# A four-layer trunk on one core: the product with the compressed values as one stacked 128-row pass, a bias table in fewer copies, small attention steps in other places

## The chip, the core and the metric

The kernel runs on one core of one Trainium2 chip. A core has five instruction queues that run beside each other: TensorE (PE, matrix products; the load of its stationary operand is listed apart as PEld), VectorE (DVE), ScalarE (ACT), GpSimd (POOL) and SyncE (SP, which here only issues DMAs). On chip there is SBUF, 128 partitions wide, and PSUM, where TensorE leaves its products. What is measured is the time of the one core in device microseconds; lower is better.

## The reference

A sequence of 256 positions of width 2048 passes two layers. Layer 0 is a gMLP mixer, a SwiGLU FFN (5632 wide) and a gated per-layer embedding. Then one set of keys and values is made for three attention branches. Layer 1 is the attention mixer with that set, and again an FFN and an embedding. All is float32. What the change touches is the attention with the compressed branch and the bias that every logit gets:

```python
def compress_blocks(t, pe, w1, w2):
    ...
    return jax.nn.gelu(flat @ w1) @ w2          # 15 blocks for each of 2 groups, 128 wide
...
lc = einsum('bghqd,bgkd->bghqk', qb, k_cmp) * scale + rel_bias_heads(rel_table, t[:, None] - cmp_end[None, :])
pc = softmax(where(mc, lc, NEG_INF)) * any(mc)
o_cmp = einsum('bghqk,bgkd->bghqd', pc, v_cmp)
...
out = gb[..., 0:1] * o_cmp + gb[..., 1:2] * o_slc + gb[..., 2:3] * o_win
```

There are 16 heads in 2 groups. A compressed key is a block of 32 positions at a stride of 16, so that there are 15 of them; the selected and the window branch see up to 256 positions here. The bias of a logit is a function of its distance and its head alone.

## The kernel before

**Products in three passes.** TensorE multiplies float32 numbers rounded to a shorter form (`F32R`). So that nothing is lost, both operands are split: ScalarE copies a number to the short form (the high part, `split`, line 117), VectorE subtracts that from the number (the rest, line 118), and `mm3` (lines 124 to 126) adds high by high, rest by high and high by rest in PSUM. Every weight block takes this way: SP loads it (`wraw`, line 172, tile `raw`), ScalarE and VectorE split it (`wh`, `wl`), TensorE uses it. In the narrow stream (mixers) four blocks of 512 KB are in flight, in the wide stream (FFN and embedding) blocks of 1 MB.

**Order.** `weave` emits a matrix product block by block and, after each block, the small attention steps that a table of strings names for this place (`PLAN`: `q3` is the product that makes the queries of heads 3 to 6, `|` parts its blocks). In it `kb0` to `kb7` and `vb0` to `vb7` are the blocks of the compression product for keys and values, `cT` the transposes ahead of them, `kh kk kt` and `vh vv` their ends, `kT` and `xT` transposes of keys and of the residual, `qT3` the transposes of the queries of the product `q3`, and `s5 t5 v5` the three steps of head 5: scores, transposes, values. A scheduler then interleaves the emitted instructions of each engine; each engine runs its own list strictly in that order and waits on semaphores.

**One head.** `scores`: nine matmuls, a DMA of the bias tile of the head (128 rows x 400, three buffers), and for each of six rows of logits one DVE and one ACT instruction; the probabilities times the gates stay in the tile `L`, 800 columns: window and selected, then 32 columns of the compressed branch (two blocks of queries, 16 each). `transposes`: eight of 128 x 128 into the PSUM banks `pa` and `pb`, which are split into `pah`, `pal`, `pbh`, `pbl`. `values`: the products with the values into the bank `pv`, two heads in one bank, the odd head ending it. The compressed branch is one `mm3` with 16 rows:

```python
mm3(po, VCh[:, g, :], VCl[:, g, :], bh[:16, par, 2:4].rearrange("p j s -> p (j s)"),
    bl[:16, par, 2:4].rearrange("p j s -> p (j s)"), False, False)
```

**The bias table.** In row p of a head's bias tile the table of that head is shifted by p. `prepare_bias` (line 349, near the end of the first mixer) writes the table of 16 heads x 528 numbers to DRAM (`d0`) and from there 128 copies of it, one for each partition (`bias_rep`, line 359). It is issued on SP's queue, in which the next entries are the loads of the first FFN's weights.

Of the kernel before, what the change touches and what calls it, by code (L numbers as in the profile page):

```python
# [16 lines left out]
SEQ = 256  # L17
# [16 lines left out]
RW = 528  # L34
SCALE = HD ** -0.5
# [47 lines left out]
def trunk_kernel(ctx: ExitStack, tc: tile.TileContext, a: dict, out: bass.AP):  # L83
# [27 lines left out]
    def f32v(t):  # L111
        return t.bitcast(F32)
# [224 lines left out]

    bias_rep = dram.tile([P, H, RW], F32, name="bias_rep")

# [9 lines left out]
    def prepare_bias(tbl, oh):  # L349

        rt = tp.tile([H, RW], F32, tag="t0", name="rt")
        for hs in (slice(0, RW // 2), slice(RW // 2, RW)):
# [7 lines left out]
                                            ap=[[0, P], [RW, H], [1, RW]]))  # L360
# [254 lines left out]
    with ExitStack() as bctx:  # L615
# [7 lines left out]
        VCh = bp.tile([16, G, HD], F32R, name="VCh")  # L623
        VCl = bp.tile([16, G, HD], F32R, name="VCl")
# [8 lines left out]
        def compress_steps(kv):  # L633
# [19 lines left out]
            def hidden():  # L653
                pt = gen_bank("hidT")
                for j in range(2):
                    nc.tensor.matmul(pt[:, j * 32:j * 32 + 30], st["hid"][:, j * P:(j + 1) * P], sel, start=True, stop=True)
                st["hidT"] = sm.tile([P, 2, 32], F32, tag="hidT", name="hidT_sb")
# [25 lines left out]
            def values():  # L683
                po = gen_bank("cmpo")
                vc = tp.tile([16, G, HD], F32, tag="t2", name="vc")
                nc.vector.memset(vc, 0.0)
                for g in range(G):
                    for j in range(2):
                        nc.tensor.matmul(po[:15, g * HD:(g + 1) * HD], st["hidT"][:, j, g * 15:(g + 1) * 15],
                               w2[:, 1, j, :], start=(j == 0), stop=(j == 1))  # L690
                nc.vector.tensor_copy(vc[:15], po[:15, :G * HD].rearrange("p (g d) -> p g d", g=G))
                split(VCh, VCl, vc)
# [77 lines left out]
        def attn_steps(h, qh, ql, e):  # L770
# [4 lines left out]
            def scores():  # L775
# [9 lines left out]
                nc.sync.dma_start(bias[:, :400], bass.AP(tensor=brv.tensor, offset=brv.offset + 127 + h * RW,  # L785
# [267 lines left out]
```

## Time and profile before

| | us |
|---|---|
| median of 3 runs (2242.64 to 2243.59) | 2242.7 |
| the profiled execution | 2247.32 |
| its span, from the first instruction to the last | 2245.4 |
| TensorE busy | 2224.8 (99%) |
| VectorE busy | 1775.4 (79%) |
| ScalarE busy | 1234.8 (55%) |

The profiled execution is some 4.6 us above the median of the timed ones; differences are worked out within the profile and then taken off the median. A matmul's record in the trace is longer than the time until the next one can start, since matmuls overlap: what one costs is read from the distance of two starts, not from its length.

### The profile page before, as it was taken

The page shows a single profiled execution, that of the slowest core. Times are in us where ns is not written, and L with a number is a line of the kernel's source. Part 1 is how long each engine was busy: PE and PEld are TensorE (multiplying, and loading weights), DVE is VectorE, ACT ScalarE, POOL GpSimd, SP SyncE. Part 2 cuts the span into 40 slices and gives each one's busy share as a digit, 9 for nine tenths or more (in the row PEclk, how much of TensorE's full clock was granted, in tenths as well). Part 3 has the DMA queues.
Part 4 walks back from the last instruction along what each step waited for, and adds up shares of the span by engine and source line. Part 5 has one row for each costly group of instructions (what it writes and reads, how often), then busy time and mean ns, then how long its engine had stood idle before and what let it go on. Part 6 is the DMA issues. An engine that isn't in the chain of part 4 may idle for free.

```text
span 2245.4 us, 26612 instructions
## 1 busy us (share of the span) xinstructions
PE 2224.8 (99%) x10311; PEld 1849.1 (82%) x10311; DVE 1775.4 (79%) x2032; ACT 1234.8 (55%) x1438; POOL 25.6 (1%) x26
## 2 busy tenths in 40 slices
PE   8999999999999999999999999999999999999999
PEld 7888878888888888888887998888888888888887
DVE  5566579998988999755667777699999998898654
ACT  7555455555555555455567666555555555555543
POOL 0000000000000000000000000000000000000000
PEclk9999999999999999999999999999999999999999
DMA  8666756566555556655557444556555656655553
GB/s 310 193 193 211 214 198 206 179 214 213 200 200 189 199 199 207 206 182 180 184 174 237 120 154 140 179 197 206 194 200 204 208 188 206 218 198 203 184 196 132
DMA packets 118570, 438.54 MB, mean 195 GB/s; under 512 B 9147, under 2 KB 11579, under 8 KB 117932
## 3 DMA queue, kind: packets, MB, share of 16 engines
q1 hardware_dynamic: 116924, 434.38, 57.8%
q10 hardware_dynamic: 1440, 2.20, 0.3%
q8 instruction: 81, 1.33, 0.2%
q14 instruction: 45, 0.37, 0.1%
q0 software_dynamic: 80, 0.26, 0.0%
HBM read 434.68 MB, written 6.46 MB: 196 GB/s over the span
## 4 chain that ended last, share of the span: by engine, by line
PE 91%; DVE 3%; DMA 3%; ACT 1%; issue 1%; POOL 0%; SPq 0%; DVEq 0%; ACTq 0%
PE p L125 12%; PE p L126 12%; PE p L124 12%; PE fo L126 7%; PE fo L124 7%; PE fo L125 7%; PE pg L126 3%; PE pg L124 3%; PE pg L125 3%; DVE wl L118 2%; DMA raw<-in_ffn_w_in 2%; PE v L124 1%; PE v L125 1%; PE v L126 1%; PE bo L124 1%; PE u L125 1%
## 5 line engine op out<-in xcount | busy, mean ns | idle before, releaser
L118 DVE TENSOR_TENSOR wl<-raw,wh 128x2048 fp32r<-128x2048 f32 (+5 forms) x513 | 876.2, 1714 | 324.3 <-ACT wh L117 322.4
L117 ACT ACTIVATE wh<-raw 128x2048 fp32r<-128x2048 f32 (+5 forms) x513 | 744.9, 1455 | 638.3 <-PE fo L126 144.0
L117 ACT ACTIVATE wh<-t 128x1024 fp32r<-128x1024 f32 x204 | 209.0, 1056 | 198.7 <-PE p L126 78.0
L118 DVE TENSOR_TENSOR wl<-t,wh 128x1024 fp32r<-128x1024 f32 x204 | 242.9, 1220 | 43.9 <-ACT wh L117 43.4
L124 PE MATMUL p<-wh,exh 128*128 128x512 f32 x470 | 183.0, 391 | 0.9 <-ACT wh L117 0.9
L125 PE MATMUL p<-wl,exh 128*128 128x512 f32 x470 | 183.4, 390 | 0.1
L126 PE MATMUL p<-wh,exl 128*128 128x512 f32 x470 | 183.3, 390 | 0.0
L125 PE MATMUL p<-wl,hF0h 128*128 128x512 f32 x418 | 163.5, 391 | 3.0 <-DVE wl L118 3.0
L125 PE MATMUL p<-wl,hF1h 128*128 128x512 f32 x418 | 162.9, 390 | 0.6 <-DVE wl L118 0.6
L126 PE MATMUL p<-wh,hF0l 128*128 128x512 f32 x418 | 162.8, 390 | 0.0
L126 PE MATMUL p<-wh,hF1l 128*128 128x512 f32 x418 | 162.4, 389 | 0.0
L124 PE MATMUL p<-wh,hF0h 128*128 128x512 f32 x418 | 161.7, 391 | 0.4 <-ACT wh L117 0.4
L124 PE MATMUL p<-wh,hF1h 128*128 128x512 f32 x418 | 161.2, 390 | 0.0
L124 PE MATMUL fo<-wh,aT0h 128*128 128x512 f32 x352 | 138.3, 393 | 0.0
L124 PE MATMUL fo<-wh,aT1h 128*128 128x512 f32 x352 | 138.2, 393 | 0.0
L126 PE MATMUL fo<-wh,aT1l 128*128 128x512 f32 x352 | 137.2, 390 | 0.0
L126 PE MATMUL fo<-wh,aT0l 128*128 128x512 f32 x352 | 137.2, 390 | 0.0
L125 PE MATMUL fo<-wl,aT1h 128*128 128x512 f32 x352 | 137.1, 390 | 0.0
L125 PE MATMUL fo<-wl,aT0h 128*128 128x512 f32 x352 | 137.1, 389 | 0.0
L490 DVE TENSOR_TENSOR t<-raw 128x1024 f32<-128x1024 f32 x102 | 124.3, 1219 | 5.6 <-DMA raw<-in_ffn_w_in 5.6
L124 PEld LDWEIGHTS p<-wh,exh 128*128 128x128 f32 x470 | 88.4, 188 | 21.0 <-ACT wh L117 2.9
L125 PEld LDWEIGHTS p<-wl,exh 128*128 128x128 f32 x470 | 88.4, 188 | 19.6 <-DVE wl L118 1.0
(282 smaller groups left out, 4183.2 us busy)
## 6 DMA issues: line engine op xcount, KB each, us to landing
raw<-in_ffn_w_in SPq DMA_DIRECT2D x176, 1024.0 KB, 4.9
raw<-in_ffn_w_out SPq DMA_DIRECT2D x88, 1024.0 KB, 5.0
raw<-in_ple_gate SPq DMA_DIRECT2D x32, 1024.0 KB, 4.9
raw<-in_a_w_in SPq DMA_DIRECT2D x63, 512.0 KB, 4.0
raw<-in_a_w_out SPq DMA_DIRECT2D x32, 512.0 KB, 4.2
raw<-in_b_w_out SPq DMA_DIRECT2D x32, 512.0 KB, 3.6
raw<-in_kv_w SPq DMA_DIRECT2D x24, 512.0 KB, 3.6
raw<-in_b_w_in SPq DMA_DIRECT2D x24, 384.0 KB, 3.7
```

What stands on the lines that cost most here:

```text
L117: nc.scalar.activation(hi, src, AF.Copy)
L118: nc.vector.tensor_tensor(lo, src, f32v(hi), ALU.subtract)
L124: nc.tensor.matmul(ps, lh, rh, start=start, stop=False)
L125: nc.tensor.matmul(ps, lh, rl, start=False, stop=False)
L126: nc.tensor.matmul(ps, ll, rh, start=False, stop=stop)
L490: nc.vector.tensor_tensor(t13, r[:, 1:3], r[:, 0:1].to_broadcast([P, 2, NC]), ALU.subtract)
```

## The change

It does three things. First, the compressed values are stacked: rows 0 to 31 hold the high part, rows 32 to 63 the rest, rows 64 to 95 the high part again (`VC`, made from three copies of the hidden layer, `rep`). The compressed probabilities are written three times into 96 columns of `L`, so that a transpose puts them into the same rows; there rows 0 to 63 of `bh` are high parts and rows 64 to 95 are overwritten with the rest. One matmul over 128 rows then adds the three products. For that VectorE gets one instruction more per head (32 x 256) while its `pbl` gets half as wide, and the factor on the compressed logits is 96 columns wide and not 32. The matmul stands last in the step. Second, `bias_rep` holds 32 copies and a head's bias tile comes with four DMAs of 32 rows. Third, the table of the order has the small steps at other places.

```diff
+BC = 32
...
-    "q0": "cT0 | cT1 |  kb0 kb1 | kb2 kb3 | kb4 | kb5 kb6 | kb7  | kh kk",
-    "q3": "kt vb0 | vb1 vb2 | qT0 vb3 | vb4 s0 vb5 | s1 vb6 | vb7 t0 | vh s2 | vv  v0",
+    "q0": "cT0 |  | kb0 kb1 | kb2 kb3 | cT1 kb4 | kb5 | kb6 kb7 | kh kk",
+    "q3": "vb0 | vb1 | qT0 kt vb2 vb3 s0 | vb4 vb5 | s1 vb6 | vb7 t0 | s2 | vh vv v0",
...
-    bias_rep = dram.tile([P, H, RW], F32, name="bias_rep")
+    bias_rep = dram.tile([BC, H, RW], F32, name="bias_rep")
...
         nc.sync.dma_start(bias_rep, bass.AP(tensor=d0v.tensor, offset=d0v.offset,
-                                            ap=[[0, P], [RW, H], [1, RW]]))
+                                            ap=[[0, BC], [RW, H], [1, RW]]))
...
+                    rep = st["rep"] = tp.tile([P, 2, G, P], F32, tag="t2", name="rep")
+                    nc.vector.memset(rep, 0.0)
+                    for j in range(2):
+                        nc.scalar.activation(rep[:, j].rearrange("p g (i m) -> p g i m", i=4)[:, :, :3, :15],
+                                             pt[:, j * 32:j * 32 + 30].rearrange("p (g m) -> p g m", g=G).unsqueeze(2)
+                                             .to_broadcast([P, G, 3, 15]), AF.Gelu_apprx_tanh)
...
-                vc = tp.tile([16, G, HD], F32, tag="t2", name="vc")
-                nc.vector.memset(vc, 0.0)
...
-                        nc.tensor.matmul(po[:15, g * HD:(g + 1) * HD], st["hidT"][:, j, g * 15:(g + 1) * 15],
-                               w2[:, 1, j, :], start=(j == 0), stop=(j == 1))
-                nc.vector.tensor_copy(vc[:15], po[:15, :G * HD].rearrange("p (g d) -> p g d", g=G))
-                split(VCh, VCl, vc)
+                        nc.tensor.matmul(po[:, g * HD:(g + 1) * HD], st["rep"][:, j, g, :],
+                                         w2[:, 1, j, :], start=(j == 0), stop=(j == 1))
+                pov = po[:, :G * HD].rearrange("p (g d) -> p g d", g=G)
+                nc.scalar.activation(VC, pov, AF.Copy)
+                nc.vector.tensor_tensor(VC[32:64], pov[32:64], f32v(VC[32:64]), ALU.subtract)
...
-                nc.sync.dma_start(bias[:, :400], bass.AP(tensor=brv.tensor, offset=brv.offset + 127 + h * RW,
-                                                         ap=[[H * RW - 1, P], [1, 400]]))
+                for p0 in range(0, P, BC):
+                    nc.sync.dma_start(bias[p0:p0 + BC, :400],
+                                      bass.AP(tensor=brv.tensor, offset=brv.offset + 127 - p0 + h * RW,
+                                              ap=[[H * RW - 1, BC], [1, 400]]))
...
-                nc.vector.tensor_tensor(LC, LC, rr[:, 4:6].unsqueeze(2).to_broadcast([P, 2, 16]), ALU.mult)
+                nc.vector.tensor_tensor(L[:, 512:608].rearrange("p (i b s) -> p i b s", i=3, b=2),
+                                        LC.unsqueeze(1).to_broadcast([P, 3, 2, 16]),
+                                        rr[:, 4:6].unsqueeze(1).unsqueeze(3).to_broadcast([P, 3, 2, 16]), ALU.mult)
...
-                split(pair["bh"][:, par].rearrange("p j s -> p (j s)"),
-                      pair["bl"][:, par].rearrange("p j s -> p (j s)"), pb)
+                bh = pair["bh"][:, par].rearrange("p j s -> p (j s)")
+                nc.scalar.activation(bh, pb, AF.Copy)
+                nc.vector.tensor_tensor(bh[64:96, SEQ:], pb[64:96, SEQ:], f32v(bh[64:96, SEQ:]), ALU.subtract)
+                nc.vector.tensor_tensor(pair["bl"][:, par].rearrange("p j s -> p (j s)"), pb[:, :SEQ],
+                                        f32v(bh[:, :SEQ]), ALU.subtract)
...
-                mm3(po, VCh[:, g, :], VCl[:, g, :], bh[:16, par, 2:4].rearrange("p j s -> p (j s)"),
-                    bl[:16, par, 2:4].rearrange("p j s -> p (j s)"), False, False)
...
+                nc.tensor.matmul(po, VC[:, g, :], bh[:, par, 2:4].rearrange("p j s -> p (j s)"),
+                                 start=False, stop=par == 1)
```

The change moves every line below it, so that `mm3` stands in lines 126 to 128 of the changed kernel. Three places show what becomes of the lists.

TensorE, the value step of the last head, before (`pv` is the bank of two heads, `pah` and `pbh` transposed probabilities, `bo` the next matrix product):

```order
L126 MATMUL pv<-pah,Vl 128x256
L124 MATMUL pv<-pbh,VCh 128x256
L125 MATMUL pv<-pbl,VCh 128x256
L126 MATMUL pv<-pbh,VCl 128x256
L124 MATMUL pv<-pbh,Vh 128x2x128
L125 MATMUL pv<-pbl,Vh 128x2x128
L126 MATMUL pv<-pbh,Vl 128x2x128
L124 MATMUL pv<-pbh,Vh 128x2x128
```

and in the changed kernel:

```order
L128 MATMUL pv<-pah,Vl 128x256
L126 MATMUL pv<-pbh,Vh 128x2x128
L127 MATMUL pv<-pbl,Vh 128x2x128
L128 MATMUL pv<-pbh,Vl 128x2x128
L126 MATMUL pv<-pbh,Vh 128x2x128
L127 MATMUL pv<-pbl,Vh 128x2x128
L128 MATMUL pv<-pbh,Vl 128x2x128
L874 MATMUL pv<-pbh,VC 128x256
L126 MATMUL bo_0_10566<-wh,oTh 128x512
```

Three entries with `VCh` and `VCl` are gone, one with `VC` stands at the end.

TensorE, in the product `q3`, where the queries of heads 0 to 2 are transposed (`qT`), before (`ph` is the compression product, `kcT` the transposed compressed keys):

```order
L647 MATMUL ph<-wh,T 128x256
L648 MATMUL ph<-wl,T 128x256
L894 MATMUL qT<-ident,q 128x128 x6
L647 MATMUL ph<-wh,T 128x256
L125 MATMUL q_0_8936<-wl,hBh 128x512
L126 MATMUL q_0_8936<-wh,hBl 128x512
```

and in the changed kernel:

```order
L128 MATMUL q_0_8935<-wh,hBl 128x512
L126 MATMUL q_1_8936<-wh,hBh 128x512
L127 MATMUL q_1_8936<-wl,hBh 128x512
L128 MATMUL q_1_8936<-wh,hBl 128x512
L914 MATMUL qT<-ident,q 128x128 x6
L688 MATMUL kcT<-ident,kc 128x30
L651 MATMUL ph<-wl,T 128x256
```

Between the end of `q0` and `qT` there now stand 36 matmuls of `q3` and 17 of `ph` (before 26 and 24), and `kcT`, which stood 30 matmuls ahead of `qT`, comes behind it. The scores of head 0 stood 38 matmuls behind `qT` and now stand 16 behind it.

SP, the loads for the last query product and the first blocks of `bo` (its weight is `in_b_w_out`), before:

```order
L172 DMA raw<-in_b_w_in 128x768 x2
L172 DMA raw<-in_b_w_out 128x1024 x4
L785 DMA bias<-bias_rep 128x400
L172 DMA raw<-in_b_w_out 128x1024
L785 DMA bias<-bias_rep 128x400
L172 DMA raw<-in_b_w_out 128x1024
L785 DMA bias<-bias_rep 128x400
```

and in the changed kernel:

```order
L174 DMA raw<-in_b_w_out 128x1024 x5
L797 DMA bias<-bias_rep 32x400 x6
L174 DMA raw<-in_b_w_out 128x1024
L797 DMA bias<-bias_rep 32x400 x4
L174 DMA raw<-in_b_w_out 128x1024 x2
L797 DMA bias<-bias_rep 32x400 x2
```

Where one bias load stood between two weight loads there now stand two to six pieces.

## Rows read from the trace of the kernel before

**Rows 1.** The profile's page: each engine's busy time, share of the span and instructions.

```profile
PE 2224.8 (99%) x10311; PEld 1849.1 (82%) x10311; DVE 1775.4 (79%) x2032; ACT 1234.8 (55%) x1438; POOL 25.6 (1%) x26
```

**Rows 2.** TensorE's waits over the whole span: who waited for whom, us in total, times, longest.

```profile
PE p L125 <- DVE wl L118: 3.7, 5, 1.8
PE qT L894 <- DVE q L882: 1.0, 1, 1.0
```

**Rows 3.** Stretches of the span: from:to, their length, busy time of PE, PEld, DVE, ACT, POOL with instructions, granted TensorE clock, DMA share, GB/s. The first lies at the start of the first FFN, the second holds the end of `q0` and all of `q3`, the third the products `q7` to `q13`, the fourth most of the blocks of `bo` that attention steps are woven into.

```profile
290.00:300.00 10.00, 7.72 (x30) 5.92 (x29) 8.53 (x11) 8.13 (x11) 0.00 (x0) 0.83 0.53 203
...
1170.00:1235.00 65.00, 61.53 (x355) 52.95 (x353) 48.59 (x99) 47.59 (x84) 3.20 (x2) 1.00 0.71 229
1235.00:1330.00 95.00, 95.00 (x602) 89.23 (x603) 75.07 (x235) 65.96 (x180) 4.91 (x3) 1.00 0.44 132
1330.00:1400.00 70.00, 69.89 (x369) 57.98 (x368) 50.20 (x120) 42.93 (x104) 1.64 (x1) 1.00 0.44 140
```

**Rows 4.** TensorE in order of time in the value step of the last head: start, us, line, rows*columns of the stationary operand, shape of the moving one.

```profile
1383.39 0.28 PE L125 MATMUL pv<-pal,Vh 128*128 128x256 f32 x1
1383.51 0.28 PE L126 MATMUL pv<-pah,Vl 128*128 128x256 f32 x1
1383.72 0.38 PE L124 MATMUL pv<-pbh,VCh 16*128 16x256 f32 x1
1383.94 0.27 PE L125 MATMUL pv<-pbl,VCh 16*128 16x256 f32 x1
1384.06 0.28 PE L126 MATMUL pv<-pbh,VCl 16*128 16x256 f32 x1
1384.26 0.39 PE L124 MATMUL pv<-pbh,Vh 128*128 128x256 f32 x1
1384.49 0.28 PE L125 MATMUL pv<-pbl,Vh 128*128 128x256 f32 x1
```

**Rows 5.** The instructions on the tile `VCh`, one group for all heads: count, ns min/median/max, first and last start.

```profile
L124 PE MATMUL pv<-pbh,VCh x16: 377/382/383, 1236.7 to 1383.7; 16*128 16x256 f32 x16
```

**Rows 6.** TensorE in order of time in the value step of head 1, in which a transpose (L822) stands between the 16-row matmuls; left out are those three and one of 128 rows.

```profile
1242.55 0.28 PE L126 MATMUL pv<-pah,Vl 128*128 128x256 f32 x1
...
1243.06 0.33 PE L822 MATMUL pa<-ident,L 128*128 128x128 f32 x1
...
1243.96 0.28 PE L125 MATMUL pv<-pbl,Vh 128*128 128x256 f32 x1
```

**Rows 7.** The way to the first FFN: SP's queue in order of time at the write of the bias copies, the list of DMA issues with KB and us from issue to landing, and, out of the chain of work that ended last, the load of FFN weights issued at 276.11 us (start, us until it landed).

```profile
267.52 0.57 SPq L359 DMA_DIRECT2D bias_rep<-d  x1
...
bias_rep<-d SPq DMA_DIRECT2D x1, 4224.0 KB, 18.5
...
276.11 13.21 DMA raw<-in_ffn_w_in
```

**Rows 8.** ScalarE and TensorE in order of time at the start of the first FFN; in brackets the idle time before and its releaser. `p` are the FFN's first products, `mT` the first transposes behind them.

```profile
285.43 0.63 ACT L233 ACTIVATE junk<-x_sb 128x512 f32<-128x512 f32 x1 [0.64 <-DVE x_sb L304]
289.41 1.92 ACT L117 ACTIVATE wh<-raw 128x2048 fp32r<-128x2048 f32 x1 [3.25 <-DMA raw<-in_ffn_w_in]
...
284.45 0.39 PE L124 MATMUL p<-wh,hF0h 128*128 128x512 f32 x1
...
289.89 1.04 PE L264 MATMUL xT<-ident,x_sb 128*128 128x128 f32 x8
291.38 0.50 PE L124 MATMUL p<-wh,hF0h 128*128 128x512 f32 x1 [0.45 <-ACT wh L117]
293.71 0.50 PE L125 MATMUL p<-wl,hF0h 128*128 128x512 f32 x1 [1.83 <-DVE wl L118]
...
335.83 1.03 PE L313 MATMUL mT<-ident,up 128*128 128x128 f32 x8
```

**Rows 9.** The same place in the second layer's FFN: the two loads issued at 1432.2 us (KB, us to landing), and TensorE from the first product to the first `mT`.

```profile
raw<-in_ffn_w_in SPq DMA_DIRECT2D x2, 1024.0 KB, 6.0
...
1440.54 0.39 PE L124 MATMUL p<-wh,hF1h 128*128 128x512 f32 x1
1440.77 0.39 PE L125 MATMUL p<-wl,hF1h 128*128 128x512 f32 x1
...
1487.46 1.03 PE L313 MATMUL mT<-ident,up 128*128 128x128 f32 x8
```

**Rows 10.** TensorE in order of time from the last matmul of `q0` to the query transposes.

```profile
1191.31 0.35 PE L126 MATMUL q<-wh,hBl 128*128 128x432 f32 x1
...
1198.85 0.21 PE L676 MATMUL kcT<-ident,kc 30*128 30x30 f32 x1 [0.19 <-DVE kc L672]
...
1204.89 1.14 PE L894 MATMUL qT<-ident,q 128*128 128x128 f32 x6 [0.96 <-DVE q L882]
```

**Rows 11.** VectorE's instructions on `pbl` and on `L` that the change alters, or that are nearest to its new ones: ns min/median/max, shapes.

```profile
L118 DVE TENSOR_TENSOR pbl<-pb,pbh x16: 670/681/685, 1227.4 to 1382.7; 128x512 fp32r<-128x512 f32 x16
...
L813 DVE TENSOR_TENSOR L<-L,rr x16: 405/418/420, 1220.0 to 1370.4; 128x256 f32<-128x256 f32 x16
L814 DVE TENSOR_TENSOR L<-L,rr x16: 173/184/186, 1220.3 to 1370.7; 128x32 f32<-128x32 f32 x16
```

**Rows 12.** The instructions on the tile `bias`: SP's issue of one load (ns), and us from issue to landing.

```profile
L785 SPq DMA_DIRECT2D bias<-bias_rep x16: 326/327/425, 1092.7 to 1330.5; - x16
...
DMA to landing us min/median/max: 2.4/2.5/5.6
```

More of the change, by code (lines that the diff above doesn't have):

```diff
@@ L622, in trunk_kernel @@
         Vl = bp.tile([P, 2, TT, G, HD], F32R, name="Vl")
-        VCh = bp.tile([16, G, HD], F32R, name="VCh")
-        VCl = bp.tile([16, G, HD], F32R, name="VCl")
+        VC = bp.tile([P, G, HD], F32R, name="VC")
         brv = bias_rep[:, :, :]
@@ L656, in hidden @@
                     nc.tensor.matmul(pt[:, j * 32:j * 32 + 30], st["hid"][:, j * P:(j + 1) * P], sel, start=True, stop=True)
+                if kv == 1:
+                    rep = st["rep"] = tp.tile([P, 2, G, P], F32, tag="t2", name="rep")
[4 more added lines that the diff above has]
+                                             .to_broadcast([P, G, 3, 15]), AF.Gelu_apprx_tanh)
+                    return
                 st["hidT"] = sm.tile([P, 2, 32], F32, tag="hidT", name="hidT_sb")
@@ L784, in scores @@
                 bias = at.tile([P, 416], F32, tag="bias", name="bias", align_bytes=128, bufs=3)
-                nc.sync.dma_start(bias[:, :400], bass.AP(tensor=brv.tensor, offset=brv.offset + 127 + h * RW,
-                                                         ap=[[H * RW - 1, P], [1, 400]]))
-                L = at.tile([P, 800], F32, tag="L", name="L", align_bytes=128)
+                for p0 in range(0, P, BC):
+                    nc.sync.dma_start(bias[p0:p0 + BC, :400],
+                                      bass.AP(tensor=brv.tensor, offset=brv.offset + 127 - p0 + h * RW,
+                                              ap=[[H * RW - 1, BC], [1, 400]]))
+                L = at.tile([P, 896], F32, tag="L", name="L", align_bytes=128)
                 L1 = L[:, :512].rearrange("p (k b s) -> p k b s", k=2, b=2)
-                LC = L[:, 512:544].rearrange("p (b s) -> p b s", b=2)
-                L0 = L[:, 544:800].rearrange("p (b s) -> p b s", b=2)
+                LC = L[:, 864:896].rearrange("p (b s) -> p b s", b=2)
+                L0 = L[:, 608:864].rearrange("p (b s) -> p b s", b=2)
                 s1v = s1.rearrange("p (k b s) -> p k b s", k=2, b=2)
@@ L821, in transposes @@
                 for b in range(2):
-                    nc.tensor.transpose(pa[:, b * SEQ:b * SEQ + P], L[:, 544 + b * P:544 + (b + 1) * P], ident)
+                    nc.tensor.transpose(pa[:, b * SEQ:b * SEQ + P], L[:, 608 + b * P:608 + (b + 1) * P], ident)
                     nc.tensor.transpose(pa[:, b * SEQ + P:(b + 1) * SEQ], L[:, b * P:(b + 1) * P], ident)
@@ L829, in transposes @@
                     pair["bh"] = at.tile([P, 2, 4, P], F32R, tag="pbh", name="pbh", align_bytes=128, bufs=1)
-                    pair["bl"] = at.tile([P, 2, 4, P], F32R, tag="pbl", name="pbl", align_bytes=128, bufs=1)
+                    pair["bl"] = at.tile([P, 2, 2, P], F32R, tag="pbl", name="pbl", align_bytes=128, bufs=1)
                 st["pah"] = pah = at.tile([P, 2, SEQ], F32R, tag="pah", name="pah", align_bytes=128)
@@ L855, in values @@
                         mm3(pb_out, Vh[:, b, 1, g, :], Vl[:, b, 1, g, :], bh[:, :, b], bl[:, :, b],
-                            False, b == 1)
+                            False, False)
+                nc.tensor.matmul(po, VC[:, g, :], bh[:, par, 2:4].rearrange("p j s -> p (j s)"),
+                                 start=False, stop=par == 1)
+                if par == 1:
                     split(oT[0][:, h - 1:h + 1, :].rearrange("p k s -> p (k s)"),
```

12 rows, old and new, of the table PLAN are left out of this document.

## The prediction

> **What bounds the kernel now.** I began with the page. TensorE is busy in 2224.8 us, 99% of the span [rows 1]; the others have slack on average. So time can be won in two ways only: fewer or shorter slots on TensorE, and the few places where it stands still. Next I read its waits over the whole span: the longest entries after the start-up are short, 3.7 us in five pieces in the first products of the FFN and 1.0 us at the query transposes [rows 2]. Then the windows, stage by stage. In the attention part, 1235 to 1330 us, TensorE has no idle time, VectorE is busy 75.07 of 95 and ScalarE 65.96; between 1330 and 1400 it is 69.89 of 70 [rows 3]. Between 1170 and 1235 TensorE is busy 61.53 of 65: here work waits. And at 290 to 300 us it is busy 7.72 of 10, at a granted clock of 0.83 where nearly everywhere else it is 1.00 [rows 3]. The change has a part in each of these places.
>
> A busy TensorE hides one thing that the timeline shows: how far apart two starts lie. That is the price of a matmul here, and with it I cost the first part.
>
> **The stacked product.** In the last head's value step, 128-row matmuls of 256 columns start 0.12 us apart (1383.39, 1383.51). Then come the three 16-row ones. The first starts 0.21 later, the second 0.22 after it, the third 0.12, and the next two 128-row ones after 0.20 and 0.23 [rows 4]. Going to the short operand and back each costs about 0.2 us over the plain distance. From 1383.51 to 1384.49 are 0.98 us; two of the starts in it are 128-row matmuls at 0.12. So the three compressed passes cost 0.98 - 0.24 = 0.74 us, although their columns are worth 0.36. There are 16 such groups, one per head [rows 5]: 16 x 0.74 = 11.8. In three heads the lists put another matmul between the 16-row ones, which makes one more change each way. In head 1 the stretch is 1.41 us [rows 6], of which three foreign starts are 0.34: 1.07, that is 0.33 more. Three such heads add 1.0. In all 12.8 us. The new pass has 128 rows like its neighbours, so neither change is left: 16 x 0.12 = 1.9. The term is 1.9 - 12.8 = **-10.9 us**. Its bounds: if the new pass, the last of its group, still cost a change on one side (0.2), it would be 16 x 0.2 = 3.2 less, -7.7; if all foreign matmuls were dearer than I count them, -11.9.
>
> The Trainium skill (TensorEngine Tiling (Array Packing), Performance Considerations, When to Use Tiling) advises the opposite of stacking for a contract dimension of 32 or less: four row tiles side by side. By that the three 16-row passes would be worth about one pass, and making them one full pass would win next to nothing. The row differs: these three read the same rows 0 to 15, start 0.22 and 0.12 us apart and not together, and pay at both ends.
>
> What the new form adds lies on VectorE. `pbl` took 0.681 us at 512 columns [rows 11]; it becomes two instructions. No row shows either: at half of it they are 0.68 together, and with each at the 0.418 of a 256-column instruction 0.84, so 0 to 0.16 more. The factor on the compressed logits goes from 32 to 96 columns, between 0.184 and 0.418 [rows 11], on the line between them 0.25. So at most some 0.2 to 0.4 us per head, 3 to 6 in all, in a stage in which VectorE has about 20 of 95 us free and TensorE never waits [rows 3]. I cost it at nothing; the cover is that slack. The `rep` and `VC` instructions replace the four on `vc`; nothing.
>
> **Fewer bias copies.** The write of `bias_rep` is issued at 267.52 and takes 18.5 us to land, to 286.0. A load of FFN weights is issued in its middle, at 276.11, and lands 13.21 us later [rows 7]. ScalarE has been ready for it since its last `junk` at 285.43, and starts the split only at 289.41, when the load is there [rows 8]. TensorE has by then only the eight transposes of 289.89 left and waits 0.45 and 1.83 us; behind the pause the clock falls, which the window's 0.83 shows [rows 3, 8]. The second layer has the same code and no bias write: its loads land in 6.0 us, and TensorE goes from its first product to `mT` in 1487.46 - 1440.54 = 46.92 us [rows 9]. Here it is 335.83 - 284.45 = 51.38 [rows 8]. So 4.5 us are there to be won. A quarter of the copies at the same rate lands in 18.5 / 4 = 4.6 us, at about 272, ahead of the loads. They are then there at some 282; ScalarE is held until 286.2 by `junk`, splits until 288.1, VectorE until 290.4. TensorE needs the rest-part at about 290.9, so it just fits. I take **-4.1 us**, a little less than the second layer shows, since there the split began before the last `junk`. Bounds: 0 if the load is late for another reason, -4.9 if a later wait of the same FFN goes too.
>
> **The steps moved.** `q0` ends with the matmul of 1191.31; the queries are ready for their transposes at 1204.89, where TensorE has waited 0.96 us (0.19 for `kcT` before) [rows 10]. That moment is set by ScalarE, VectorE and GpSimd, and TensorE's waits before it are swallowed by it. The change puts ahead of it 36 matmuls of `q3` and 17 of `ph` in place of 26 and 24: at 0.23 [rows 9] and 0.12 us that is 10.3 against 8.9, 1.4 us more of work that is needed anyway. So the wait there goes: **-1.4 us**. On the other side the scores of head 0 now stand 16 matmuls, 1.9 us, behind these transposes, and in between the transposed queries must be split on ScalarE and VectorE, beside other blocks. That may cost 0.5 us; the other waits of this stretch (61.53 of 65 busy [rows 3] leaves some 2 us) are as dense in blocks as before, and I let them stand. Bounds -4 to +3. The distances between scores, transposes and values of one head elsewhere are no shorter in the lists where they were short, so I expect no new stalls from 1235 on.
>
> **Four DMAs for one.** An issue costs SP 0.327 us, a bias tile landed in 2.5 [rows 12]. 48 more issues are 48 x 0.327 = 15.7 us of SP's time, spread over some 300 us; the tiles have three buffers, and of weights four blocks are under way. I cost it at nothing; the cover is these buffers. The Trainium skill (SBUF — State Buffer, The DMA setup-cost knee) speaks against the split: every transfer pays about 2 us whatever its size. By it, an estimate, a head's four pieces would take 8 us if they came one by one; the trace of before has no such small piece, and by that sum nothing follows for TensorE as long as the tile is three heads ahead.
>
> **The sum.** -10.9 - 4.1 - 1.4 = -16.4 us: the profile's execution would be 2247.3 - 16.4 = 2230.9, and off the median 2242.7, which lies 4.6 lower, **2226 us**.
>
> **Rivals.**
> - *The FFN's first load stays late.* For it: the load waits for an SBUF buffer until 276.11, bias or not. Against: the second layer's, gated alike, lands in 6.0. Time 2242.7 - 10.9 - 1.4 = 2230.
> - *VectorE becomes the bound between the heads.* TensorE's stage of 95 us loses about 7, VectorE's 75 gets 2 more: 77 of 88. On average it fits; but in the first FFN's start VectorE is at 8.53 of 10 with TensorE waiting. If half of the stacked product's gain and the moved steps' are given back in waits, 2242.7 - 5.5 - 4.1 = 2233.
> - *The stack does not do what it says*: the cost at both ends comes from the switch of accumulation, not from the rows, and stays: only the two passes go, 32 x 0.12 = 3.8. 2242.7 - 3.8 - 4.1 - 1.4 = 2233.
> - *Slower: pieces of bias hold up weights in SP's queue.* SP goes in order, and up to six pieces stand between two weight loads; a piece that waits for a buffer or an earlier landing holds the weights behind it. A block takes about 4 us in this stage (36 blocks in 150 us), three are ahead, 12; landing and split take some 6. So a head's pieces may hold the queue 6 us longer than the one load did. Above that, TensorE waits: it decides at 7.3 us (16.4 / 13 heads behind the first three = 1.3 over the slack). Four pieces one by one at the longest landing, 5.6 [rows 12], less 2.5 are 20 us, 14 over the slack: if that met one head 2242.7 - 16.4 + 14 = 2240, two 2254. Against: the median landing, 2.5, gives 7.5, just at the edge, and several pieces may be under way at once.
>
> **How the numbers follow.** The forecast 0.62, the FFN's load 0.12, VectorE 0.10, the stack 0.07, SP 0.05 (half of it slower than before), and 0.04 for a stall of the moved steps that I don't see. The forecast's own range, by the bounds of its terms, is 2221 to 2231. The three cases that give part back end at 2233; with the SP case partly in, 2219 to 2237 leaves no more than 2 in 10 out. 0.2% of 2242.7 is 4.5 us, about what a measurement of this kernel can tell from no change: faster means under 2238.2. Of the cases all but SP and the unseen stall end there: 0.92; within 0.2%: 0.05; slower: 0.03.
>
> **What would show it.** `pv<-pbh,VC` at 0.12 us from its neighbours on both sides, with no record of 16 rows left. The `bias_rep` write landing in 5 to 6 us, no wait and a clock of 1.00 at the first FFN products, and about 47 us from there to `mT`. The query transposes without a wait. Wrong would be: TensorE waiting for `wl` or `wh` between 1235 and 1400, with a weight load behind bias pieces in SP's list; or a value step as long as before.

## The result, and the profile after

The changed kernel takes 2230.5 us (median of 4 runs, 2229.3 to 2233.7) against 2243.1 for the kernel before: a ratio of 0.9945, interval 0.9933 to 0.9957, that is 12.6 us less (9.6 to 15.0). It is faster, inside the forecast range of 2219 to 2237, and 4.5 us above the forecast of 2226. The profiled execution took 2229.6 us, with a span of 2227.8. Of all executions in this document, one of the bias part alone and one of the kernel before were far slower at a lower granted clock (0.75 and 0.48); they enter no ratio.

The page of the changed kernel, engine by engine as in [rows 1], and some of TensorE's waits, as in [rows 2] (who waited for whom: us in total, times, longest):

```profile
PE 2210.3 (99%) x10279; PEld 1842.7 (83%) x10279; DVE 1776.1 (80%) x2047; ACT 1235.0 (55%) x1439; POOL 26.2 (1%) x26
...
PE ph L651 <- DVE wl L120: 1.4, 2, 1.2
PE pv L127 <- DVE pbl L854: 0.9, 1, 0.9
...
PE p L127 <- DVE wl L120: 0.7, 2, 0.5
PE pb L840 <- DVE ql L123: 0.5, 1, 0.5
```

TensorE has 32 matmuls fewer and 14.5 us less busy time. The FFN's wait for `wl` went from 3.7 to 0.7 us, and that of the query transposes is gone. The longest wait of all, 6.1 us at `v`, is the start-up's; before has one of 6.4. New are `pv` waiting for `pbl` (0.9), `pb` waiting for `ql` (0.5), and a longer wait of `ph`.

Now the stretches of [rows 3] in the changed kernel, same columns (from:to, length, busy time of PE, PEld, DVE, ACT, POOL, granted TensorE clock, DMA share, GB/s):

```profile
290.00:300.00 10.00, 10.00 (x46) 8.26 (x45) 9.93 (x15) 6.26 (x11) 0.00 (x0) 1.00 0.55 210
...
1170.00:1235.00 65.00, 62.22 (x363) 54.14 (x362) 49.32 (x106) 49.11 (x94) 4.44 (x3) 1.00 0.68 222
1235.00:1330.00 95.00, 93.47 (x605) 89.38 (x604) 81.67 (x256) 69.00 (x188) 5.83 (x4) 1.00 0.44 137
```

At the first FFN TensorE is busy all the time at a clock of 1.00. Between 1235 and 1330 it now idles 1.5 us, where before it never did.

TensorE in order of time around the stacked pass of a late head (start, us, line), as in [rows 4], and the tile `VC`'s group, the answer to [rows 5]:

```profile
1366.35 0.29 PE L127 MATMUL pv<-pbl,Vh 128*128 128x256 f32 x1
1366.47 0.28 PE L128 MATMUL pv<-pbh,Vl 128*128 128x256 f32 x1
1366.59 0.28 PE L874 MATMUL pv<-pbh,VC 128*128 128x256 f32 x1
1366.71 0.40 PE L126 MATMUL bo<-wh,oTh 128*128 128x512 f32 x1
...
L874 PE MATMUL pv<-pbh,VC x16: 276/282/388, 1231.0 to 1366.6; 128*128 128x256 f32 x16
```

The pass starts 0.12 us behind its neighbour, and the next matmul 0.12 behind it. 0.74 us have become 0.12.

The way to the first FFN, in the order of [rows 7] and [rows 8]: SP's queue, the DMA issues (KB, us to landing), ScalarE, and TensorE's first product and first `mT`:

```profile
265.79 0.56 SPq L361 DMA_DIRECT2D bias_rep<-d  x1
275.26 1.57 SPq L174 DMA_DIRECT2D raw<-in_ffn_w_in  x2
...
raw<-in_ffn_w_in SPq DMA_DIRECT2D x2, 1024.0 KB, 6.7
bias_rep<-d SPq DMA_DIRECT2D x1, 1056.0 KB, 5.5
...
285.21 3.71 ACT L119 ACTIVATE wh<-raw 128x2048 fp32r<-128x2048 f32 x2
...
283.60 0.39 PE L126 MATMUL p<-wh,hF0h 128*128 128x512 f32 x1
...
330.52 1.03 PE L315 MATMUL mT<-ident,up 128*128 128x128 f32 x8
```

The write is over at 271.3, before the loads are issued; these land 5.0 and 8.3 us after their issue (6.7 is the median), the first at 280.3, and ScalarE splits at 285.21 with no wait. From the first product to `mT` are 46.92 us, to a hundredth what the second layer took [rows 9].

The query transposes, to be held against [rows 10]: they follow the product before them by 0.23 us, with no wait.

```profile
1197.19 0.40 PE L128 MATMUL q<-wh,hBl 128*128 128x512 f32 x1
1197.42 0.92 PE L914 MATMUL qT<-ident,q 128*128 128x128 f32 x6
```

Last, VectorE's changed instructions (ns min/median/max), against [rows 11], and SP's on `bias` with the landing times, against [rows 12]:

```profile
L854 DVE TENSOR_TENSOR pbl<-pb,pbh x16: 423/425/426, 1220.9 to 1364.3; 128x256 fp32r<-128x256 f32 x16
L828 DVE TENSOR_TENSOR L<-L,rr x16: 248/251/253, 1212.2 to 1356.7; 128x96 f32<-128x96 f32 x16
...
L797 SPq DMA_DIRECT2D bias<-bias_rep x64: 302/419/1735, 1086.7 to 1321.7; - x64
...
DMA to landing us min/median/max: 1.7/3.3/5.0
```

With the 0.42 us of the other new one (`pbh`, L853) the two instructions take 0.16 us more than the old `pbl`, the factor on `L` 0.07 more: 16 x 0.23 = 3.7 us in all, inside the 3 to 6 of the prediction.

### The profile page after: what moved, and what is told of

It reads as the page before. It is cut to its first block, busy times and chain, and to the rows that moved or that the text cites. A ratio compares the mean times of both kernels' runs of the same rounds, so it can differ in the third digit from the quotient of the medians.

```text
span 2227.8 us, 26621 instructions
## 1 busy us (share of the span) xinstructions
PE 2210.3 (99%) x10279; PEld 1842.7 (83%) x10279; DVE 1776.1 (80%) x2047; ACT 1235.0 (55%) x1439; POOL 26.2 (1%) x26
## 4 chain that ended last, share of the span: by engine, by line
PE 93%; DVE 3%; DMA 1%; ACT 1%; issue 1%; POOL 0%; SPq 0%; DVEq 0%; ACTq 0%; POOLq 0%
PE p L127 13%; PE p L128 13%; PE p L126 12%; PE fo L128 7%; PE fo L127 7%; PE fo L126 7%; PE pg L128 3%; PE pg L126 3%; PE pg L127 3%; DVE wl L120 1%; PE v L126 1%; PE v L127 1%; PE v L128 1%; PE ao L128 1%; PE bo L128 1%; PE bo L127 1%
```

## The experiments

One number recurs: the length of a stage in TensorE's own time, from the first matmul of one product to the first of the next, so that what happened before a stage does not enter it. `p` is the first FFN's first product up to `mT`; `q0`, `q3`, `q7` (with `q10` and `q13`) and `bo` are the stretches with attention steps. The lists move steps from one stage into another, so two kernels with different lists are compared by the sum of these four, in the last column. In us, one profiled execution each:

| kernel | p | q0 | q3 | q7 | bo | q0 to bo |
|---|---|---|---|---|---|---|
| before | 51.38 | 29.21 | 43.22 | 95.18 | 109.63 | 277.24 |
| before again | 49.31 | 29.06 | 43.34 | 95.17 | 109.59 | 277.16 |
| three passes of 128 rows | 47.86 | 29.39 | 43.36 | 91.18 | 107.53 | 271.46 |
| bias part alone | 46.93 | 29.19 | 42.59 | 95.19 | 109.64 | 276.61 |
| stack alone | 48.90 | 30.12 | 42.37 | 89.35 | 106.86 | 268.70 |
| lists alone | 48.15 | 28.77 | 40.61 | 94.73 | 110.37 | 274.48 |
| after | 46.92 | 28.31 | 41.08 | 90.80 | 106.65 | 266.84 |
| after, old lists | 46.93 | 29.45 | 43.63 | 90.16 | 106.92 | 270.16 |
| after, 128 copies | 47.36 | 28.14 | 41.00 | 90.80 | 106.64 | 266.58 |
| after again | 46.93 | 28.08 | 40.55 | 90.83 | 106.64 | 266.10 |
| after, three 128-row passes | 46.92 | 28.51 | 41.03 | 91.77 | 108.07 | 269.38 |

Theory 1 is the prediction's account: the stack wins because the changes between 16-row and 128-row passes go, the FFN's loads were late because of the bias write, and the lists remove the wait of `qT`. The rivals stand in each expectation.

### The kernel before, once more

No edit. It asks what the profiled execution, 4.6 us above its median, had of its own.

> The kernel before, unchanged, to see how far one execution stands for the others. Theory 1 (the prediction's terms hold in every execution): the wait of some 4.2 us at the start of the first FFN (0.45 and 1.83 us idle, then a clock of 0.5 for 3.4 us) is there again, and the span is within 1 us of 2245.4. Theory 2 (the wait belongs to the one execution that was profiled, which was 4.6 us above the median): the span is about 2241, and the way from the first FFN product to mT takes about 47 us, not 51.4.

2244.0 us beside 2244.3, ratio 0.9999 (0.9990 to 1.0008). The same rows as before (bias write, loads, the split on ScalarE, the window):

```profile
bias_rep<-d SPq DMA_DIRECT2D x1, 4224.0 KB, 17.8
raw<-in_ffn_w_in SPq DMA_DIRECT2D x2, 1024.0 KB, 13.1
...
288.50 1.92 ACT L117 ACTIVATE wh<-raw 128x2048 fp32r<-128x2048 f32 x1 [2.18 <-DMA raw<-in_ffn_w_in]
...
290.00:300.00 10.00, 8.53 (x42) 6.92 (x41) 9.43 (x13) 7.26 (x11) 0.00 (x0) 1.00 0.56 213
```

The first load takes 12.14 us where it took 13.21 [rows 7] (13.1 is the median of the two; before, 14.2), ScalarE waits 2.18 us instead of 3.25, and TensorE's clock stays at 1.00. `p` is 49.31, not 51.38: neither theory's number. The low clock of [rows 3] belonged to that one execution: in it the granted clock lay at 0.5, 1.2 GHz, for 3.4 us behind the wait of 1.83 us, which by itself is 1.7 us of the 4.5 that the prediction set out to win.

### Three passes of 128 rows in the old kernel

```diff
-        VCh = bp.tile([16, G, HD], F32R, name="VCh")
-        VCl = bp.tile([16, G, HD], F32R, name="VCl")
+        VCh = bp.tile([P, G, HD], F32R, name="VCh")
+        VCl = bp.tile([P, G, HD], F32R, name="VCl")
...
-                vc = tp.tile([16, G, HD], F32, tag="t2", name="vc")
+                vc = tp.tile([P, G, HD], F32, tag="t2", name="vc")
...
-                mm3(po, VCh[:, g, :], VCl[:, g, :], bh[:16, par, 2:4].rearrange("p j s -> p (j s)"),
-                    bl[:16, par, 2:4].rearrange("p j s -> p (j s)"), False, False)
+                mm3(po, VCh[:, g, :], VCl[:, g, :], bh[:, par, 2:4].rearrange("p j s -> p (j s)"),
+                    bl[:, par, 2:4].rearrange("p j s -> p (j s)"), False, False)
```

The same three passes with the same accumulation, only 128 rows instead of 16, the rest zeros. Nothing on VectorE grows but the two one-off instructions on `vc`.

> The kernel before, with VCh and VCl filled up with zeros to 128 rows, so that the compressed product is still three passes, but of 128 rows each; nothing else changes. Theory 1 (the cost at both ends of the group is that of going to 16 rows and back): a group costs 3 x 0.12 = 0.36 us and not 0.74, 16 x 0.38 + 1.0 = 7.1 us less, 2236. Rival (the cost belongs to the group of accumulations, whatever its rows): no change, 2243.

2236.9 us, ratio 0.9970 (0.9958 to 0.9982): 7.4 us less by the medians, 6.7 by the ratio. The number of passes has not changed, so the price at both ends comes from the rows, not from the accumulation, and the rival on that is refuted. But TensorE now waits in value steps. One head of this kernel, TensorE and VectorE in order of time (idle before and releaser in brackets):

```profile
1299.86 0.28 PE L124 MATMUL pv<-pbh,VCh 128*128 128x256 f32 x1
1301.76 0.39 PE L125 MATMUL pv<-pbl,VCh 128*128 128x256 f32 x1 [0.74 <-DVE pbl L118]
...
1300.08 1.03 DVE L882 SCALAR_TENSOR_TENSOR q<-q,rq 128x384 f32<-128x384 f32 x2 [1.23 <-POOL rq L156]
1301.03 0.68 DVE L118 TENSOR_TENSOR pbl<-pb,pbh 128x512 fp32r<-128x512 f32 x1
```

`pbl` is behind the scaling of the queries in VectorE's queue, and that stood 1.23 us waiting for GpSimd's `rq`; TensorE then waits 0.74 us for `pbl`. In the kernel before, the same head has the same order in VectorE's queue:

```profile
1308.53 0.38 PE L125 MATMUL pv<-pbl,VCh 16*128 16x256 f32 x1
...
1306.84 1.03 DVE L882 SCALAR_TENSOR_TENSOR q<-q,rq 128x384 f32<-128x384 f32 x2 [1.22 <-POOL rq L156]
1307.79 0.68 DVE L118 TENSOR_TENSOR pbl<-pb,pbh 128x512 fp32r<-128x512 f32 x1
```

VectorE waited as long there, and `pbl` was ready at 1308.47, 0.06 us before TensorE came to it. The padding made TensorE's steps ahead shorter and left VectorE's as they were. In `q7` and `bo` this kernel gains 6.1 us. By the starts in the kernel before, the 16 groups lie 7.4 us over three plain passes each (the prediction's prices say 7.0); two waits of `pv` give 1.3 of that back.

### The bias part alone

```diff
-    bias_rep = dram.tile([P, H, RW], F32, name="bias_rep")
+    bias_rep = dram.tile([BC, H, RW], F32, name="bias_rep")
...
-                nc.sync.dma_start(bias[:, :400], bass.AP(tensor=brv.tensor, offset=brv.offset + 127 + h * RW,
-                                                         ap=[[H * RW - 1, P], [1, 400]]))
+                for p0 in range(0, P, BC):
+                    nc.sync.dma_start(bias[p0:p0 + BC, :400],
+                                      bass.AP(tensor=brv.tensor, offset=brv.offset + 127 - p0 + h * RW,
+                                              ap=[[H * RW - 1, BC], [1, 400]]))
```

> The kernel before with the bias part alone: 32 copies, four DMAs for a bias tile. Theory 1: 4.1 us less, 2239, with no wait at the first FFN products. Theory 2: the wait is not there in most executions anyway, and the pieces cost nothing: 2242 to 2243. Rival (pieces hold up weights): over 2244, with waits for weights between 1235 and 1400 us.

2242.9 us, ratio 0.9994 (0.9985 to 1.0002): 1.4 us less, not clear of nothing. The mechanism is there: the write lands in 5.6 us, the loads in 8.5, `p` is 46.93. `q7` and `bo` are 95.19 and 109.64, as in before: the 48 added DMAs cost nothing that shows.

### The stack alone

The changed kernel with `BC = 128` (one bias load per head) and the old lists.

> The changed kernel with the old order of the small steps, 128 bias copies and one DMA for a bias tile: the stacked product alone. Theory 1: 10.9 us less than before, 2232. Rival (VectorE's extra work between the heads is felt): 2234 to 2238, with waits for pbl or L in the attention stage.

2235.7 us, ratio 0.9963 (0.9951 to 0.9975): 8.6 us less, where the term says 10.9. The chief waits in question (us in total, times, longest):

```profile
PE hidT L659 <- issue: 1.1, 1, 1.1
PE qT L914 <- DVE q L902: 1.0, 1, 1.0
...
PE pv L127 <- DVE pal L120: 0.8, 1, 0.8
PE pv L127 <- DVE pbl L854: 0.6, 2, 0.4
```

Before has no wait of `pv`, and 0.3 us at `hidT`. The longer wait at `hidT` is made up behind it: `q0` and `q3` together take 72.49 us, in the two executions of before 72.43 and 72.40. All of the gain is in `q7` and `bo`, 196.21 for 204.81, and there `pv` waits at four places. The longest, TensorE and VectorE:

```profile
1272.52 0.34 PE L128 MATMUL q<-wh,hBl 128*128 128x384 f32 x1
1273.68 0.39 PE L127 MATMUL pv<-pal,Vh 128*128 128x256 f32 x1 [0.82 <-DVE pal L120]
...
1270.82 0.56 DVE L902 SCALAR_TENSOR_TENSOR q<-q,rq 128x384 f32<-128x384 f32 x1 [1.43 <-POOL rq L158]
```

The two starts lie 1.16 us apart where 0.17 is plain: 0.99 us are lost for an idle time of 0.82. At the four places 0.60, 0.99, 0.20 and 0.32 are lost in this way, 2.1 us. -10.9 + 2.1 = -8.8: the term as worked out, less waits that it had not. At each of the four the scaling of the queries had waited 0.79 to 1.43 us for `rq` ahead of the tile that TensorE needs.

### The lists alone

The kernel before with the new `PLAN`, nothing else.

> The kernel before with the new order of the small steps alone. Theory 1: the wait of 1 us at the query transposes goes, 1.4 us less, 2242. Rival (the new places make waits of their own): 2243 to 2247, with waits of TensorE between 1190 and 1275 us that the kernel before does not have.

2240.3 us, ratio 0.9985 (0.9976 to 0.9994): 3.3 us less, over twice the predicted 1.4. `q0` to `bo` take 274.5 us where before took 277.2, 2.7 less. `q3` alone falls from 43.3 to 40.6, but 1.6 of that is no gain: 14 of its matmuls (their plain distances) stand in later stages now. The row of the query transposes has no wait, as expected; another wait, at `cmpo`, is longer than in either execution of before (0.2 and 0.6):

```profile
1201.70 0.91 PE L894 MATMUL qT<-ident,q 128*128 128x128 f32 x6
...
PE cmpo L664 <- ACT hidT_sb L658: 1.4, 1, 1.4
```

In the repeat of before the start distances at `qT` and right behind it lie 1.4 us over the plain ones, here 0.2. Two more products of `q3` that waited for `wl` there (0.5 each over the plain distance) do not wait here. And one part of the gain is none of the lists' own: in head 1, where a transpose stood between the 16-row matmuls [rows 6], they now follow one another:

```profile
1238.13 0.28 PE L126 MATMUL pv<-pah,Vl 128*128 128x256 f32 x1
...
1239.10 0.27 PE L125 MATMUL pv<-pbl,Vh 128*128 128x256 f32 x1
```

The stretch is 0.97 us; before it was 1.41, of which 0.34 were the three foreign starts. Of three heads with such a group one is left, and over all 16 groups the starts lie 6.4 us over plain passes instead of 7.4. The prediction has this 1.0 us in the stack's term, and a kernel with the stack can win it only once.

### The changed kernel with the old lists, with 128 copies, and again

The first puts the old `PLAN` back into the changed kernel. The second writes all 128 copies and keeps the four-piece loads:

```diff
-    bias_rep = dram.tile([BC, H, RW], F32, name="bias_rep")
+    bias_rep = dram.tile([P, H, RW], F32, name="bias_rep")
...
-                                            ap=[[0, BC], [RW, H], [1, RW]]))
+                                            ap=[[0, P], [RW, H], [1, RW]]))
```

The third is the changed kernel unchanged.

> The changed kernel with the old order of the small steps: stack and bias part. Theory 1: 1.4 us slower than the changed kernel, 2232, and 15 less than before. Rival (the new order is what lost some of the forecast): 2226 to 2228, faster than the changed kernel.

> The changed kernel, but 128 copies of the bias table are written to DRAM as before; the tiles still come in four pieces from the first 32 of them. It tells the write from the pieces. Theory 1: the wait at the first FFN products is back, 4.1 us slower than the changed kernel, 2234 to 2235. Theory 2 (that wait is not there in most executions): the same as the changed kernel, 2230.

> The changed kernel unchanged, to see how its executions spread (four gave 2229.3 to 2233.7, while four of the kernel before gave 2242.6 to 2243.6) and where the trace of another execution differs. If the spread comes from the waits between 1180 and 1280 us, these differ between its two traces by as much as the spans do.

2233.5, 2232.3 and 2231.1 us, ratios 0.9953 (0.9939 to 0.9966), 0.9952 (0.9940 to 0.9965) and 0.9943 (0.9930 to 0.9955). The lists are worth 2.4 us, the copies 1.2, and each interval overlaps that of the third, so the stages must say it: `q0` to `bo` are 270.16 with the old lists, 266.84 and 266.10 with the new; `p` is 47.36 with 128 copies and 46.92 or 46.93 with 32. With the old lists `pv` waits at four places again, 2.2 us, with the new ones at one, 0.9. The two traces of the changed kernel have spans of 2227.8 and 2227.6, though their `q0` and `q3` differ by 0.8 us: the spread does not come from the waits between 1180 and 1280 alone. The rows of the 128 copies:

```profile
bias_rep<-d SPq DMA_DIRECT2D x1, 4224.0 KB, 17.2
raw<-in_ffn_w_in SPq DMA_DIRECT2D x2, 1024.0 KB, 11.2
...
287.12 1.92 ACT L119 ACTIVATE wh<-raw 128x2048 fp32r<-128x2048 f32 x1 [0.21 <-DMA raw<-in_ffn_w_in]
```

The same write, and yet ScalarE waits only 0.21 us for the load, where the profiled before waited 3.25.

### More work for VectorE in the changed kernel

```diff
+                more = at.tile([P, SEQ], F32, tag="more", name="more")
+                nc.vector.tensor_copy(more, pb[:, :SEQ])
                 nc.vector.tensor_tensor(pair["bl"][:, par].rearrange("p j s -> p (j s)"), pb[:, :SEQ],
```

A copy that nobody reads, ahead of `pbl` in every head. It separates the amount of VectorE's work from its order.

> The changed kernel with one VectorE instruction more for each head, a copy of 128 x 256 out of PSUM into a tile that nobody reads, behind the 32-row subtraction: some 0.4 us, 6.6 us in all on VectorE. Theory 1 (VectorE has slack between the heads): within 1 us of the changed kernel, 2230 to 2231. Rival (the value steps wait for VectorE, which is what held back part of the stack's gain): each head's wait grows, 2233 to 2237.

2232.2 us, ratio 0.9951 (0.9938 to 0.9965). The 16 copies and the one wait of `pv` for `pbl`:

```profile
L855 DVE COPY more<-pb x16: 424/425/426, 1220.4 to 1364.3; 128x256 f32<-128x256 f32 x16
...
1236.88 0.38 PE L127 MATMUL pv<-pbl,Vh 128*128 128x256 f32 x1 [1.26 <-DVE pbl L856]
```

The time lies between the two forecasts: 6.8 us more on VectorE cost 1.6 by the medians (intervals overlap) and 0.6 in `q7` and `bo` (198.02 for 197.45). The one place that waited in the changed kernel waits 0.36 us longer, about one copy; in one other head a wait of 0.2 for `pal` comes up. The amount of VectorE's work is not the bound.

### Three passes of 128 rows in the changed kernel

The changed kernel with the old `VCh`, `VCl`, `pbl` and `L`, padded to 128 rows as above; bias and lists as changed.

> The changed kernel with three passes of 128 rows (zeros filled in) in place of the stack; VectorE's instructions are those of the kernel before. Theory 1 (TensorE's slots alone decide): 16 x 2 x 0.12 = 3.8 us slower than the changed kernel, 2234 to 2235. Rival (the stack's added VectorE work costs in the value steps): 2231 to 2232, with shorter waits for pbl than the changed kernel has.

2234.7 us, ratio 0.9960 (0.9948 to 0.9973): 4.2 us over the changed kernel by the medians and 3.4 by the ratios, against 32 passes x 0.12 = 3.8. In `q7` and `bo` it is 2.4 (199.84 for 197.45), since the waits there are shorter: it has VectorE's old instructions, and `pv` waits once, 0.5 us, for `pal`, where the changed kernel waits 0.9 for `pbl` and 0.5 at `pb`. So the new instructions may lengthen the waits, but a wait is there without them; the lists alone, with the longer 16-row passes, have none at `pv`.

### Two other lists

Two tries to take the waits left in `q0` to `q7`. In the first `kh kk` go a block later, `v1` one, and `t6` away from right behind `qT7`; the second has the first step alone:

```diff
-    "q0": "cT0 |  | kb0 kb1 | kb2 kb3 | cT1 kb4 | kb5 | kb6 kb7 | kh kk",
-    "q3": "vb0 | vb1 | qT0 kt vb2 vb3 s0 | vb4 vb5 | s1 vb6 | vb7 t0 | s2 | vh vv v0",
-    "q7": "t1 | v1 t2 | v2 qT3 | s3 s4 | t3 | s5 v3 | t4 | t5 s6",
-    "q10": "v4 |  | qT7 v5 t6 | s7 v6 | s8 | t7 |  | s9 v7",
+    "q0": "cT0 |  | kb0 kb1 | kb2 kb3 | cT1 kb4 | kb5 | kb6 kb7 | ",
+    "q3": "kh vb0 | kk vb1 | qT0 vb2 kt vb3 s0 | vb4 vb5 | s1 vb6 | vb7 t0 | s2 | vh vv v0",
+    "q7": "t1 |  | v1 t2 | v2 qT3 | s3 s4 | t3 | s5 v3 | t4",
+    "q10": "t5 v4 s6 |  | qT7 v5 | t6 s7 | v6 s8 | t7 |  | s9 v7",
```

> The changed kernel with the steps moved once more, away from the waits that its trace shows: kh and kk (the ends of the compression of the keys) one block later, the values of head 1 one block behind its transposes, the transposes of head 6 one block behind the query transposes. Theory 1: the waits for hidT, cmpo, pbl and ql, 2 to 3 us, go: 2228. Rival (the waits move on to other steps): 2230 to 2232.

> The first of the three moves of k1_plan alone (kh and kk one block later). Theory 1: the waits for hidT and cmpo at the start of q3, 0.75 to 1.7 us, go: 2229.5. Rival (they are swallowed by the later wait of the query transposes or the scores of head 0): 2230 to 2231.

2229.5 us, ratio 0.9938 (0.9926 to 0.9951), and 2230.4, ratio 0.9943 (0.9930 to 0.9955). Neither is clear of the changed kernel. In the first the waits of `hidT`, `ph` and `cmpo` are gone, that of `pv` for `pbl` is 0.5, `t6` waits 0.6 for `L` instead of 0.5 for `ql`, and others have come: 1.7 us for a `wl` in `q` and 1.1 for the first scores' `KTh`. In the second `hidT` and `cmpo` are gone too, and a wait of 1.4 for `wl` in `q` has come. The work of these stages is dense enough that a step moved gives one wait for another.

## Why the prediction was right or wrong

| term | predicted | alone | the step |
|---|---|---|---|
| stack | -10.9 | -8.6 | price of the passes right, waits behind them missed |
| bias copies | -4.1 | -1.4 | mechanism right, size taken from one execution |
| lists | -1.4 | -3.3 | the wait named is gone, two others with it; 1.0 belongs to the stack's term |
| sum | -16.4 | -13.3 | together measured: -12.6 |

**The stack.** Right: 0.12 us on both sides, and that the cost at both ends comes from the rows (by the prediction's prices three padded passes are worth 12.8 - 48 x 0.12 = 7.0 us, and they gained 6.7 to 7.4; over them the stack should gain 3.8, and did gain 3.4 to 4.2 with the new lists, but only 1.2 to 1.6 with the old, where the waits took the rest). The step that failed is "I expect no new stalls from 1235 on". VectorE's cover was counted as an amount, 75 of 95 us, and the amount was right: 6.8 us more of it cost 1.6 by the medians. What decides is the order in its queue, and how soon TensorE comes. At head 1 of the changed kernel, TensorE and VectorE:

```profile
1236.38 0.33 PE L127 MATMUL q<-wl,hBh 128*128 128x384 f32 x1
1237.61 0.39 PE L127 MATMUL pv<-pbl,Vh 128*128 128x256 f32 x1 [0.90 <-DVE pbl L854]
...
1235.39 1.29 DVE L902 SCALAR_TENSOR_TENSOR q<-q,rq 128x512 f32<-128x512 f32 x2 [1.02 <-POOL rq L158]
1236.70 0.42 DVE L853 TENSOR_TENSOR pbh<-pb,pbh 32x256 fp32r<-32x256 f32 x1
1237.13 0.42 DVE L854 TENSOR_TENSOR pbl<-pb,pbh 128x256 fp32r<-128x256 f32 x1
```

And the same place in the kernel before:

```profile
1241.14 0.68 DVE L118 TENSOR_TENSOR pbl<-pb,pbh 128x512 fp32r<-128x512 f32 x1
1242.98 1.29 DVE L882 SCALAR_TENSOR_TENSOR q<-q,rq 128x512 f32<-128x512 f32 x2 [1.15 <-POOL rq L156]
```

In before `pbl` is ahead of the scaling of the queries, in after behind it, with 1.02 us of waiting for GpSimd and 1.29 of work in front. The old value steps were long enough to cover such places, the new ones are not. Place alone is not enough: at 1297.36 in the changed kernel the scaling, after 1.36 us of waiting, stands right ahead of a `pbl` again, and TensorE, which needs that `pbl` later, does not wait. That the waits come without the new VectorE instructions is shown (both padded kernels). The scaling, held 0.5 to 1.4 us by `rq`, stands ahead of every wait of `pv` in the traces; that its place makes them is read from there, and no run moved it alone.

**The bias copies.** All the signs came: write in 5.5 us, no wait of ScalarE, clock 1.00, 46.92 us to `mT`. The step that failed is the size: 4.1 us was taken from the profiled execution, where `p` was 51.38, and then subtracted from the median, which belongs to other executions. The six kernels with 128 copies have a `p` of 51.38, 49.31, 47.86, 48.90, 48.15 and 47.36, 48.83 on average: 1.9 over the 46.92 or 46.93 that every kernel with 32 has. The 4.6 us between the profiled time and the median were the warning that this execution held something the others had not. The rival that the load stays late for another reason is refuted: with 32 copies it landed in 6.3 to 8.5 us, with 128 in 11.2 to 14.2.

**The lists.** The wait of `qT` went as told. The bounds of -4 to +3 held; the value was too small because "the other waits of this stretch ... I let them stand", and two of them went too, while the one at `cmpo` grew; and the 1.0 us of the two groups made whole was counted with the stack.

**The four DMAs.** Nothing, as costed: no wait of TensorE for `wl` or `wh` from 1235 on, so SP's queue held no weight back. The landing of a 50 KB piece, 1.7/3.3/5.0 us, next to 2.5 for the whole 200 KB tile before [rows 12], agrees with the fixed price per transfer that the Trainium skill states (SBUF — State Buffer, The DMA setup-cost knee) in that a quarter of the bytes landed no sooner; paid ahead of need, it cost nothing here. As to the Trainium skill's advice on short contract dimensions (TensorEngine Tiling (Array Packing), When to Use Tiling), no run here laid passes side by side on different rows; on the same rows the 16-row form lost 7 us against zeros.

**The sum.** The three parts alone add up to -13.3, or -12.3 if the 1.0 us that both stack and lists win is counted once; together they gave -12.6, so they hardly disturb one another. The forecast of -16.4 came this close in part by luck: the stack and the copies fell short by 2.3 and 2.7, and the lists, in which the prediction let things stand, gave 1.9 more. By its number the rival of the late load (2230) came nearest, but its mechanism is refuted. Of the rival of VectorE as the bound (2233) the waits came true, though not the share of half of the gain, and by the order in its queue instead of its amount of work.

**Open.** By what means the 128-copy write holds the loads back: in all six traces with it the first load lands 2.4 to 3.3 us behind the end of the write, so how long ScalarE waits goes with the write's end, and why the write took anything from 17.2 to 18.5 us is not known. Nor is why the waits of `cmpo` and `ph` in `q0` and `q3` differ from one execution of the same kernel to the next (`cmpo` 0.4 and 1.4 us in the changed kernel). They are one part of the spread; the start-up (88.9 to 90.9 us from `v` to `u`) varies by more.

## What to carry to other kernels

When TensorE is busy 99% of the time, read what a matmul costs from the distance between starts: it shows a price, here 0.4 us per group of short passes, that no busy time shows. Shortening TensorE's work brings forward all that it asks of the other engines: look in their queues at what stands ahead of the instruction it will then need, and for an instruction there that itself waits, instead of adding up their free time. And read a stall that is to be removed in more than one execution, above all when the profiled time lies above the median.

## What the runs showed of the hardware

- Three 16-row passes between 128-row ones cost 0.74 us, three 128-row passes with 112 rows of zeros 0.36 by the plain distance: filling the rows with zeros was the cheaper form by 7 us over 16 groups.
- A write of 4.2 MB from DRAM to DRAM (17.2 to 18.5 us) took the landing of 1 MB loads issued 8.6 to 9.7 us behind it from 6.3 to 8.5 us (medians of two) up to 11.2 to 14.2; the first of the two landed 2.4 to 3.3 us after the write had.
- A VectorE instruction that waited 0.5 to 1.4 us for GpSimd held what stood behind it in VectorE's queue; TensorE felt it in some places (0.03 to 1.26 us idle at `pv`) and not in others.
- TensorE's granted clock fell to 0.5 (1.2 GHz) for 3.4 us, 0.83 over the stretch of [rows 3], only in the execution with the longest wait there, 1.83 us after one of 0.45; in the repeat, with 1.5, it stayed at 1.00.
